# Retiming the per-token expert row operations of a one-core PEER decoder layer, and moving half of its weight residuals from VectorE to GpSimd

## The chip, the cores and the metric

One core of one Trainium2 chip runs one decoder layer for 512 tokens in one launch. The metric is device time in microseconds (us). The kernel before takes 3232.92 us (median of 3 runs, 3228.34 to 3236.88).

Names in the text: PE is TensorE, DVE is VectorE, ACT is ScalarE, POOL is GpSimd, SP is SyncE, which issues most of the DMAs.

## The reference, cut to what matters

x is 512 tokens of 2048 floats. The layer is

- h = rmsnorm(x); z = h W_in (2048 to 4096 columns: pool, q, k, v); a pooling mixer on the first 1024 columns, dilated causal attention with partial rotary embedding on 8 heads of 128; x += concat W_out.
- x += cross attention (4 heads, 256 memory tokens).
- PEER: 8 heads of queries (h W_pq, 2048 columns) are scored against two sets of 128 keys; the 16 best of each side are combined and the best 16 pairs name 16 of 16384 experts with softmax gates. Expert e adds gate * gelu(h . w_u[e]) * w_v[e]. So every token has 128 expert rows of w_u and 128 of w_v.
- a final rmsnorm.

## The kernel before, in words

Everything is float32. A projection is done with three matmuls per weight block: weight and activation are each split in a high part (float32r) and a low part (the rest), and high*high, high*low and low*high are added up (`mm3`, lines 145 to 148). `load_w` (lines 133 to 143) loads a 128x1024 half of a weight pair by SP, makes the high part `wh` on ACT, and the low part `wl = raw - wh` on DVE, or on the engine that `lo_eng` names. `proj_one` (150) makes one 128-column chunk of a projection: two `load_w`, 48 matmuls. `proj_four` (162) makes four chunks at once.

The tokens go two ways. The 128 tokens of the first block are handled on their own, from the start up to about 405 us; their 128x128 chosen experts are then fetched as rows. For each of the 128 choices k, `dot0` (311) gathers one row of w_u per token (an indirect DMA on POOL's queue, 128 rows of 8 KB, 1 MB) and DVE multiplies it with the activation `gx` in PSUM and sums (line 314). Then `turn0` (316) applies the GELU and the gates, and `axpy0` (324) gathers 128 rows of w_v and adds them up in `gx` on DVE (line 327); `out0` normalises and writes them. The first 64 tokens of the rest go the same way with two choices per step: 64 `dot1` and 64 `axpy1` (`start1`, `turn1`, `end1` around them). The other 320 tokens go through all 16384 experts as a dense product: 128 chunks of w_u (`a_chunk`, 996; 48 matmuls of 320 columns each), GELU, a product with a dense gate matrix, and 16 groups times 16 column blocks of w_v (lines 1164 to 1200; 24 matmuls each).

Order of the stages after 405 us, as the code has it:

- z: 28 chunks of W_in (`z_chunk`, 764), 20 of them between the parts of the attention heads, 8 with the pooling mixer; the choice of experts for the first block (`picks`) is made three steps per chunk at its beginning. The rotary embedding (`rope`, 755) is one shuffle and three tensor operations on DVE.
- W_out: 16 chunks, then the cross attention: 4 chunks of W_cq and 8 loads of W_co.
- queries: 16 chunks of W_pq; after each, `score` (963) makes two-level top 16 lists on DVE (five operations for each of 3 token blocks), and `dense_h` (976) makes the activations of the dense product.
- w_u: 128 chunks. The choices for three token blocks (`pick`) run beside the first ones; then 80 gate groups (`gates`, 1092: two DVE operations, 4 matmuls, one ACT copy) are spread over chunks up to K1 = 56. All gates must be in memory before the dense gate product of chunk 56. Chunks 56 to 63 follow without gates.
- w_v: 16 groups; during the first 8 of them the other 64 chunks of w_u are done as well.

The row operations wait in one list, `queue`. Each chunk calls `behind(rate/4)` four times: it adds to `owed` and takes that many entries from the list (333 to 338). `RATE` and `XR` hold the entries per chunk: 2.2 in z (chunks 10 to 26), 2.0 in W_out, 0.5 in W_cq, 3.0 in the queries, 0.4 from chunk 20 of w_u. In w_v the rest of the list is spread evenly, 1.3 times as dense in the first half (1157 to 1159). A gathered row lies in a buffer from `row_tile` (107): two, plus those in the list `spare` (`x0` from line 724, `rowx` from line 951).

Instructions are reordered on each engine by the compiler's list scheduler, so a DVE row operation that is written beside one weight tile may stand much earlier or later in DVE's order; POOL keeps the written order from line 1037 on. Each engine then runs its instructions strictly in order. PSUM holds `gx` (half of it), two banks `pm` and two `pa`.

Of the kernel before, what the change touches and what calls it, by code (L numbers as in the profile page):

```python
# [17 lines left out]
P = 128  # L18
# [24 lines left out]
RATE = (2.2, 2.0, 3.0, 0.4)  # L43

XR = 0.25

PK, Z0, ZE = 3, 1, 27
# [17 lines left out]
def hybrid_kernel(ctx: ExitStack, tc: tile.TileContext, a: dict, out: bass.AP):  # L65
# [28 lines left out]
    r2c = const.tile([P, TR], F32, name="r2c")  # L94
    accx = const.tile([P, TR], F32, name="accx")
# [66 lines left out]
    def proj_four(tiles, xh, xl, n=TR, order=None, lo_eng=None, rate=0):  # L162
# [165 lines left out]

    gx = [None]
# [29 lines left out]
    with tc.tile_pool(name="ep", bufs=1) as ep, tc.manual_schedule(engines={mybir.EngineType.SP}):  # L359
# [333 lines left out]
        hooks_x = [{}, {}, {4: [lambda: rstd_from(r2c, accx, TR)]}, {}]  # L693
# [43 lines left out]
    with tc.tile_pool(name="ac", bufs=1, reuse_waits="tile") as ac, tc.tile_pool(name="at", bufs=2, reuse_waits="tile") as at:  # L737
# [26 lines left out]
        def z_chunk(c):  # L764
# [5 lines left out]
            on = len(zc) > Z0 + math.ceil(17 / PK) + 2 and len(zc) < ZE  # L770
            return proj_one(a["w_in"][c], hH, hL, rate=RATE[0] if on else 0)

        for h in range(HEADS):
            ps = fill["q%d" % h] if h <= 1 else z_chunk(8 + h)
            q = at.tile([P, 16 + TR], F32, name="q", bufs=1)[:, :TR]
            V.scalar_tensor_tensor(out=q, in0=ps, scalar=DH ** -0.5, in1=rx, op0=ALU.mult, op1=ALU.mult)  # L776
            rope(q)
            ps = fill["v0"] if h == 0 else z_chunk(24 + h)
            vt = tmp2k()
            V.tensor_tensor(vt, ps, rx, op=ALU.mult)  # L780
# [4 lines left out]
            S.copy(v, pt[:, :TR])  # L785
# [6 lines left out]
            for i in range(RB):  # L792
# [6 lines left out]
                V.tensor_tensor(s[:, :n], ps[:, :n], mask[:, T - n:], op=ALU.add)  # L799
# [47 lines left out]
    with tc.tile_pool(name="xt", bufs=2, reuse_waits="tile") as xt:  # L847
# [4 lines left out]
        xtmp = lambda n=TR: xt.tile([P, TR], F32, name="xtmp", bufs=2)[:, :n]  # L852

# [15 lines left out]
        def x_scores(h):  # L869
            ps = proj_one(a["w_cq_h"][h], hH, hL, rate=XR * RATE[1])  # L870
# [54 lines left out]
        for t in range(8):  # L925
            w = load_w(a["w_co"][t]) if t >= 1 else None
# [12 lines left out]
        rstd_tok(accx, TR, out=yq)  # L939
    kvp.close()  # L940
# [21 lines left out]
    with tc.tile_pool(name="pq", bufs=2) as pq:  # L962
# [33 lines left out]
    def a_chunk(j, stay=False):  # L996
        ps = proj_one(a["w_u"][j], dH, dL, ND, lo_eng=G if j >= K1 + GRP and j % 2 == 0 or K1 + GRP > j >= KP else V)
# [12 lines left out]
    with tc.tile_pool(name="tw", bufs=1, reuse_waits="tile") as tw:  # L1010
        for b in range(RB):
# [22 lines left out]
            a_until(4 * b + 4)  # L1034
# [42 lines left out]
    owed = 0.0

    with tc.tile_pool(name="gw", bufs=2, side="right", reuse_waits="tile") as gw:
# [33 lines left out]
        for j in range(first, K1):  # L1113
# [187 lines left out]
```

## Time and profile before

| what | value |
|---|---|
| median of 3 runs | 3232.92 us |
| the profiled execution, own time | 3235.51 us |
| its span, first to last instruction | 3233.7 us |
| mean granted TensorE clock | 0.959 of full speed |
| PE busy | 2954.9 us (91%) |
| DVE busy | 2501.6 us (77%) |
| ACT busy | 1290.9 us (40%) |
| POOL busy | 1045.4 us (32%) |
| moved by DMA | 912.79 MB, mean 282 GB/s |

An engine's busy time is the time in which it ran at least one instruction; DMA issues, waits and semaphores are not counted. Matmuls overlap in PE, so a matmul's own duration is longer than the time it adds; the time that one adds is found as busy time over count in a stretch in which PE never waits. The granted clock is the share of full speed at which TensorE was allowed to run: 1.00 is 2.4 GHz, 0.50 is 1.2 GHz.

### The profile page before, as it was taken

The numbers are of one execution on the slowest core, as the hardware profiler recorded it, in microseconds if no ns is written. First come the engines' busy times: TensorE is split into PE (matmuls) and PEld (weight loads), VectorE is DVE, ScalarE is ACT, GpSimd is POOL, SyncE is SP. The second block draws the span as 40 slices with busy tenths as digits, with TensorE's granted clock in tenths as the row PEclk, the third lists the DMA queues.
The fourth block names the chain that finished last, engine by engine and source line by source line (L and its number), as shares of the span: only waits on it lengthen the run. The fifth ranks groups of instructions, "written<-read, shape, count | busy, mean of one in ns | idle before, by whom it ended". The sixth has DMA issues, their size and how long they took to land.

```text
span 3233.7 us, 47332 instructions
## 1 busy us (share of the span) xinstructions
PE 2954.9 (91%) x18311; PEld 2840.1 (88%) x18311; DVE 2501.6 (77%) x3569; ACT 1290.9 (40%) x1756; POOL 1045.4 (32%) x633
## 2 busy tenths in 40 slices
PE   7989878899998669999999999999999998898997
PEld 5868677788988669999999999999999998898897
DVE  7787899996459999978954777777677777777775
ACT  5666432233363224455543333333333332232234
POOL 0000012330002210000566555555555554444542
PEclk8999989999999889999999999999999999999998
DMA  7886749995428965555677999889899999899873
GB/s 266 288 297 213 236 155 336 345 360 201 126 93 323 333 253 168 173 170 216 227 268 286 365 383 352 333 342 347 334 343 371 350 346 345 329 354 352 341 269 104
DMA packets 243521, 912.79 MB, mean 282 GB/s; under 512 B 23488, under 2 KB 85600, under 8 KB 192224
## 3 DMA queue, kind: packets, MB, share of 16 engines
q1 hardware_dynamic: 136304, 471.21, 41.5%
q0 software_dynamic: 55296, 402.68, 31.7%
q10 hardware_dynamic: 51696, 35.88, 3.6%
q8 instruction: 144, 2.36, 0.3%
q14 instruction: 81, 0.66, 0.1%
HBM read 874.22 MB, written 35.45 MB: 281 GB/s over the span
## 4 chain that ended last, share of the span: by engine, by line
PE 64%; DVE 15%; issue 12%; DMA 5%; ACT 1%; POOL 1%; ACTq 0%; SPq 0%; DVEq 0%; POOLq 0%
PE pm L146 11%; PE pm L147 10%; PE pm L148 10%; PE pa L148 9%; PE pa L146 8%; PE pa L147 8%; DVE wl L142 3%; PE pa L1104 2%; DVE rows L314 2%; PE pm L384 1%; PE pm L385 1%; PE pm L383 1%; DVE gx L327 1%; DVE wl L130 1%; DMA rows<-in_w_u_rows_dram,sidx 1%
## 5 line engine op out<-in xcount | busy, mean ns | idle before, releaser
L141 ACT ACTIVATE wh<-wraw 128x1024 fp32r<-128x1024 f32 (+1 forms) x658 | 694.4, 1060 | 1126.9 <-PE pm L147 563.4
L142 POOL TENSOR_TENSOR wl<-wraw,wh 128x1024 fp32r<-128x1024 f32 x240 | 597.8, 2496 | 1035.2 <-ACT wh L141 961.0
L148 PE MATMUL pa<-ch,wl 128*128 128x320 f32 x2048 | 644.8, 316 | 57.1 <-DVE wl L142 53.6
L142 DVE TENSOR_TENSOR wl<-wraw,wh 128x1024 fp32r<-128x1024 f32 (+1 forms) x418 | 533.9, 1279 | 207.8 <-ACT wh L141 198.2
L146 PE MATMUL pa<-ch,wh 128*128 128x320 f32 x2048 | 645.1, 315 | 19.3 <-ACT wh L141 8.8
L147 PE MATMUL pa<-cl,wh 128*128 128x320 f32 x2048 | 643.4, 314 | 0.0
L146 PE MATMUL pm<-dH,wh 128*128 128x320 f32 x2048 | 634.8, 310 | 0.7 <-ACT ga L999 0.7
L147 PE MATMUL pm<-dL,wh 128*128 128x320 f32 x2048 | 633.5, 309 | 0.0
L148 PE MATMUL pm<-dH,wl 128*128 128x320 f32 x2048 | 632.8, 310 | 0.0
L148 PEld LDWEIGHTS pa<-ch,wl 128*128 128x128 f32 x2048 | 394.1, 193 | 66.0 <-DVE wl L142 61.9
L146 PEld LDWEIGHTS pa<-ch,wh 128*128 128x128 f32 x2048 | 394.8, 193 | 22.3 <-ACT wh L141 12.1
L146 PE MATMUL pm<-hH,wh 128*128 128x384 f32 x1024 | 362.5, 354 | 36.9 <-DVE q L776 14.7
L147 PEld LDWEIGHTS pa<-cl,wh 128*128 128x128 f32 x2048 | 394.7, 193 | 0.0
L146 PEld LDWEIGHTS pm<-dH,wh 128*128 128x128 f32 x2048 | 384.4, 188 | 1.0 <-ACT ga L999 1.0
L147 PEld LDWEIGHTS pm<-dL,wh 128*128 128x128 f32 x2048 | 384.4, 188 | 0.0
L148 PEld LDWEIGHTS pm<-dH,wl 128*128 128x128 f32 x2048 | 384.0, 188 | 0.1
L147 PE MATMUL pm<-hL,wh 128*128 128x384 f32 x1024 | 357.9, 350 | 0.0
L148 PE MATMUL pm<-hH,wl 128*128 128x384 f32 x1024 | 356.5, 349 | 0.4 <-DVE wl L142 0.4
L114 POOL DMA_INDIRECT rows<-in_w_u_rows_dram,sidx x107 | 124.3, 1161 | 671.8 <-ACT t2k L804 456.3
L1179 DVE TENSOR_TENSOR xT<-pa,xT 128x320 f32<-128x320 f32 x256 | 125.2, 489 | 198.2 <-PE pa L148 183.0
L146 PEld LDWEIGHTS pm<-hH,wh 128*128 128x128 f32 x1024 | 202.5, 198 | 45.7 <-issue 25.4
L147 PEld LDWEIGHTS pm<-hL,wh 128*128 128x128 f32 x1024 | 202.2, 197 | 0.9
(404 smaller groups left out, 4544.5 us busy)
## 6 DMA issues: line engine op xcount, KB each, us to landing
wraw<-in_w_u_dram SPq DMA_DIRECT2D x256, 512.0 KB
wraw<-in_w_v_dram SPq DMA_DIRECT2D x256, 512.0 KB
wraw<-in_w_in_dram SPq DMA_DIRECT2D x64, 512.0 KB
xT<-in_w_in_f_dram SPq DMA_DIRECT2D x63, 512.0 KB
gd<-stage SPq DMA_DIRECT2D x10, 2048.0 KB
gt<-gd ACTq DMA_DIRECT2D x32, 640.0 KB
wraw<-in_w_pq_f_dram SPq DMA_DIRECT2D x32, 512.0 KB
wraw<-in_w_out_dram SPq DMA_DIRECT2D x32, 512.0 KB
```

Of the source, the lines that this page charges most:

```text
L114: G.indirect_dma_start(out=dst, out_offset=None, in_=src, in_offset=bass.IndirectOffsetOnAxis(ap=idx, axis=0))
L130: V.tensor_tensor(wl, raw, wh.bitcast(F32), op=ALU.subtract)
L141: S.activation(wh[:, c], raw[:, c], AF.Copy)
L142: (lo_eng or V).tensor_tensor(wl[:, c], raw[:, c], wh.bitcast(F32)[:, c], op=ALU.subtract)
L146: TE.matmul(ps, wh, xh, start=start, stop=False)
L147: TE.matmul(ps, wh, xl, start=False, stop=False)
L148: TE.matmul(ps, wl, xh, start=False, stop=stop)
L314: V.tensor_tensor_reduce(out=r, in0=r, in1=gx[0], op0=ALU.mult, op1=ALU.add, scale=1.0, scalar=0.0, accum_out=sact[:, k:k + 1])
L327: V.scalar_tensor_tensor(out=gx[0], in0=r, scalar=sact[:, k:k + 1], in1=gx[0], op0=ALU.mult, op1=ALU.add)
L383: TE.matmul(ps, xh, wh, start=start, stop=False)
L1104: TE.matmul(pg[:, j], u[:, 0, j], u[:, 1, j], start=True, stop=True)
L1179: V.tensor_tensor(xT[:, dd, NS:], ps[:, :ND], xT[:, dd, NS:], op=ALU.add)
```

## The change

- `behind` issues row operations inside `tc.issue_after(anchor)`: each DVE instruction of the entry must stand in DVE's order after the last `wl` that DVE made for a weight tile (until `paced` is set false at the end of the gates). POOL's gathers are not tied.
- The list begins with `dot0` x128, `turn0`, `axpy0` x128, `out0`; the second kind (`start1` to `end1`) comes behind it. Before, the 128 `axpy0` stood at the end.
- The rates: 3.0 in z for attention chunks from the tenth on, 2.2 for the 8 pooling chunks, 2.5 in W_out, 2.0 in W_cq, 0.25 in the queries and in the first 21 chunks of w_u, 1.2 in chunks 21 to 55 and for the 8 after them.
- One more row buffer in z (in the memory of `mb`, from the eleventh chunk to the first pooling chunk), and one in W_out and the cross attention.
- `lo_eng=(V, G)`: in z, W_out, W_cq, W_co (every second tile) and w_u chunks 21 to 55, POOL makes one of two `wl`. In the queries and w_u chunks 0 to 20 POOL makes all of them (before: DVE all up to chunk 39, POOL all from 40 to 63).
- The three tensor operations of `rope` and the first multiplication of `dense_h` go to POOL. q and v lose their scaling multiplication on DVE: q is copied with a scale on ACT and `rz` enters at the mask (same instruction count there), v is copied on ACT and scaled in three ACT copies after its transposes.
- `KB` = 7: 21 chunks of w_u are written beside the picks, before 12; the gates start at chunk 21 and spread over 33 chunks.

```diff
-RATE = (2.2, 2.0, 3.0, 0.4)
-XR = 0.25
-PK, Z0, ZE = 3, 1, 27
+RATE = (3.0, 2.2, 2.5, 2.0, 0.25, 1.2)
+PK, Z0 = 3, 1
-K1, U0, GE = 56, 8, 2
-KP = 40
+K1, U0, GE = 56, 0, 2
+KB = 7
...
+    anchor = [None]
...
-            (lo_eng or V).tensor_tensor(wl[:, c], raw[:, c], wh.bitcast(F32)[:, c], op=ALU.subtract)
+            i = (lo_eng or V).tensor_tensor(wl[:, c], raw[:, c], wh.bitcast(F32)[:, c], op=ALU.subtract)
+        if (lo_eng or V) is V:
+            anchor[0] = i
...
-            wh, wl = load_w(tiles[half], lo_eng)
+            wh, wl = load_w(tiles[half], lo_eng[half] if isinstance(lo_eng, tuple) else lo_eng)
...
-    queue = [lambda k=k: dot0(k) for k in range(P)]
+    queue = [lambda k=k: dot0(k) for k in range(P)] + [turn0] + [lambda k=k: axpy0(k) for k in range(P)] + [out0]
+    paced = [True]
     def behind(n):
...
         while owed >= 1 and queue:
-            queue.pop(0)()
+            with tc.issue_after(anchor[0].ins) if paced[0] else nullcontext():
+                queue.pop(0)()
...
-            V.tensor_tensor(sh, sh, sinT, op=ALU.mult)
-            V.tensor_tensor(t[0:32], t[0:32], cosT, op=ALU.mult)
-            V.tensor_tensor(t[0:32], t[0:32], sh, op=ALU.add)
+            G.tensor_tensor(sh, sh, sinT, op=ALU.mult)
+            G.tensor_tensor(t[0:32], t[0:32], cosT, op=ALU.mult)
+            G.tensor_tensor(t[0:32], t[0:32], sh, op=ALU.add)
...
-            on = len(zc) > Z0 + math.ceil(17 / PK) + 2 and len(zc) < ZE
-            return proj_one(a["w_in"][c], hH, hL, rate=RATE[0] if on else 0)
+            n = len(zc) - Z0 - math.ceil(17 / PK) - 2
+            if n == 2:
+                spare.append(alloc_mb()[:, :D])
+            if c == 0:
+                spare.pop()
+            return proj_one(a["w_in"][c], hH, hL, lo_eng=(V, G), rate=0 if n <= 0 else RATE[1] if c < 8 else RATE[0])
...
-            V.scalar_tensor_tensor(out=q, in0=ps, scalar=DH ** -0.5, in1=rx, op0=ALU.mult, op1=ALU.mult)
+            S.activation(q, ps, AF.Copy, scale=DH ** -0.5)
...
-            V.tensor_tensor(vt, ps, rx, op=ALU.mult)
+                S.copy(vt, ps)
...
-        for c, ps in enumerate(proj_four(a["w_pq4"], hH, hL, rate=RATE[2])):
+        for c, ps in enumerate(proj_four(a["w_pq4"], hH, hL, lo_eng=G, rate=RATE[4])):
...
-        ps = proj_one(a["w_u"][j], dH, dL, ND, lo_eng=G if j >= K1 + GRP and j % 2 == 0 or K1 + GRP > j >= KP else V)
+        lo = G if j < RB * KB else (V, G) if j < K1 else G if j < K1 + GRP or j % 2 == 0 else V
+        ps = proj_one(a["w_u"][j], dH, dL, ND, lo_eng=lo, rate=RATE[4] if j < RB * KB else RATE[5] if j < K1 else 0)
...
-            a_until(4 * b + 4)
+            a_until(KB * b + KB)
...
-    queue += [start1] + [lambda k=k: dot1(k) for k in range(NK)] + [turn1] + [lambda k=k: axpy1(k) for k in range(NK)]
-    queue += [end1, turn0] + [lambda k=k: axpy0(k) for k in range(P)] + [out0]
-    owed = 0.0
+    queue += [start1] + [lambda k=k: dot1(k) for k in range(NK)] + [turn1] + [lambda k=k: axpy1(k) for k in range(NK)] + [end1]
...
-            if j >= first + U0:
-                behind(RATE[3])
+    paced[0] = False
```

## Rows read from the trace of the kernel before

**Rows 1.** The page, part 4: chain that ended last, shares by engine

```profile
PE 64%; DVE 15%; issue 12%; DMA 5%; ACT 1%; POOL 1%; ACTq 0%; SPq 0%; DVEq 0%; POOLq 0%
```

**Rows 2.** Busy time by stretch: PE, PEld, DVE, ACT, POOL (instructions), clock, DMA share, GB/s

```profile
405.00:772.00 367.00, 306.84 (x1597) 284.17 (x1598) 341.57 (x544) 116.64 (x201) 92.52 (x75) 0.90 0.79 294
772.00:890.00 118.00, 117.78 (x680) 117.49 (x679) 51.83 (x60) 39.75 (x49) 0.00 (x0) 1.00 0.42 130
890.00:985.00 95.00, 91.19 (x499) 84.87 (x498) 61.11 (x112) 60.98 (x118) 0.94 (x1) 1.00 0.32 101
985.00:1217.00 232.00, 166.77 (x907) 163.40 (x906) 228.35 (x549) 66.41 (x118) 57.69 (x51) 0.86 0.83 310
1217.00:1381.00 164.00, 163.30 (x1116) 163.01 (x1115) 153.62 (x419) 67.70 (x84) 0.00 (x0) 1.00 0.54 172
1381.00:1669.00 288.00, 285.22 (x2095) 284.41 (x2095) 239.51 (x230) 158.64 (x176) 86.93 (x35) 1.00 0.60 208
...
1722.00:2668.00 946.00, 917.94 (x6162) 915.30 (x6161) 674.18 (x616) 323.15 (x391) 521.46 (x308) 0.98 0.91 349
2668.00:3100.00 432.00, 383.61 (x2465) 374.35 (x2464) 335.06 (x336) 129.12 (x159) 205.04 (x122) 0.96 0.91 342
3100.00:3234.00 134.00, 112.31 (x747) 110.42 (x745) 82.29 (x120) 56.55 (x102) 43.16 (x22) 0.91 0.47 159
```

**Rows 3.** DVE's instruction groups by shape, 985 to 1217 us (queries)

```profile
L314 DVE CUSTOM_DVE_ANT_0 rows<-rows,gx 128x2048 f32<-128x2048 f32 x28 | 65.2, 2337 | 0.0
L142 DVE TENSOR_TENSOR wl<-wraw,wh 128x1024 fp32r<-128x1024 f32 x34 | 43.0, 1268 | 1.1 <-ACT wh L141 1.0
L314 DVE CUSTOM_DVE_ANT_0 rowx<-rowx,gx 128x2048 f32<-128x2048 f32 x14 | 32.7, 2335 | 1.6 <-DMA rowx<-in_w_u_rows_dram,sidx 1.6
L314 DVE CUSTOM_DVE_ANT_0 x<-x,gx 128x2048 f32<-128x2048 f32 x13 | 30.4, 2335 | 0.0
```

**Rows 4.** PE's waits, 985 to 1217 us: total us, times, longest

```profile
PE pa L969 <- ACT qh L966: 60.5, 10, 14.9
```

**Rows 5.** DVE's instruction groups by shape, 405 to 772 us (z)

```profile
L314 DVE CUSTOM_DVE_ANT_0 rows<-rows,gx 128x2048 f32<-128x2048 f32 x47 | 107.0, 2276 | 5.6 <-DMA rows<-in_w_u_rows_dram,sidx 5.6
L142 DVE TENSOR_TENSOR wl<-wraw,wh 128x1024 fp32r<-128x1024 f32 x52 | 63.1, 1214 | 6.3 <-ACT wh L141 6.3
L314 DVE CUSTOM_DVE_ANT_0 x<-x,gx 128x2048 f32<-128x2048 f32 x25 | 57.0, 2278 | 6.5 <-DMA x<-in_w_u_rows_dram,sidx 6.5
L758 DVE TENSOR_TENSOR t2k<-t2k,sinT 32x384 f32<-32x384 f32 x16 | 8.6, 539 | 0.1
```

**Rows 6.** The page, part 3: DMA queues, share of 16 engines' span

```profile
q1 hardware_dynamic: 136304, 471.21, 41.5%
q0 software_dynamic: 55296, 402.68, 31.7%
```

**Rows 7.** POOL's waits, 405 to 772 us: total us, times, longest

```profile
POOL rows L114 <- DVE sact L314: 99.3, 36, 4.8
```

**Rows 8.** POOL's instruction groups, 3100 to 3234 us: a 384-column operation

```profile
L1205 POOL TENSOR_TENSOR xT<-xT,rf 128x384 f32<-128x384 f32 x5 | 6.4, 1319 | 15.1 <-ACT rf L206 15.1
```

**Rows 9.** ACT's instructions of line 999 (one per chunk), 1381 to 1669 us

```profile
L999 ACT ACTIVATE ga<-pm x30: 416/419/440, 1382.8 to 1660.3; 128x320 f32<-128x320 f32 x30
```

**Rows 10.** DVE's gate operations, 1400 to 1510 us (no tensor operation on POOL)

```profile
L1099 DVE TENSOR_TENSOR u<-iota,e12T 128x1024 f32<-128x1024 f32 x34 | 40.9, 1221 | 4.3 <-PE pa L1104 4.3
...
L1101 DVE TENSOR_TENSOR u<-u,gT 128x512 f32<-128x512 f32 x32 | 21.3, 688 | 0.4
```

**Rows 11.** DVE's gate operations, 1520 to 1660 us (POOL makes low parts)

```profile
L1099 DVE TENSOR_TENSOR u<-iota,e12T 128x1024 f32<-128x1024 f32 x41 | 71.8, 1768 | 15.3 <-PE pa L1104 15.3
L1101 DVE TENSOR_TENSOR u<-u,gT 128x512 f32<-128x512 f32 x41 | 48.9, 1209 | 0.7
```

**Rows 12.** POOL's low parts, 1520 to 1660 us

```profile
L142 POOL TENSOR_TENSOR wl<-wraw,wh 128x1024 fp32r<-128x1024 f32 x28 | 76.1, 2716 | 398.1 <-ACT wh L141 398.1
```

**Rows 13.** DVE's low parts, 1217 to 1381 us (picks beside w_u)

```profile
L142 DVE TENSOR_TENSOR wl<-wraw,wh 128x1024 fp32r<-128x1024 f32 x46 | 56.4, 1226 | 10.1 <-ACT wh L141 10.1
```

More of the change, by code (lines that the diff above doesn't have):

```diff
@@ L1 @@
 import math
-from contextlib import ExitStack
+from contextlib import ExitStack, nullcontext
 import numpy as np
@@ L94, in hybrid_kernel @@
     r2c = const.tile([P, TR], F32, name="r2c")
+    rz = const.tile([P, NB], F32, name="rz")[:, :RB]
     accx = const.tile([P, TR], F32, name="accx")
@@ L169, in proj_four @@
             if kk == 0:
-                w = load_w(tiles[t], lo_eng)
+                w = load_w(tiles[t], lo_eng[t % 2] if isinstance(lo_eng, tuple) else lo_eng)
             behind(rate / 4)
@@ L327, in axpy0, with out0 @@
         V.scalar_tensor_tensor(out=gx[0], in0=r, scalar=sact[:, k:k + 1], in1=gx[0], op0=ALU.mult, op1=ALU.add)
+    def out0():
+        sq, so = row_tile(), nrm.tile([P, 2], F32, name="so")
+        S.activation(sq, gx[0], AF.Square, accum_out=so[:, 0:1])
+        newton(so[:, 0:1], so[:, 1:2])
+        grow = row_tile()
+        nc.scalar.dma_start(grow, a["g_rows"][1:2, :].broadcast_to([P, D]))
+        V.scalar_tensor_tensor(out=grow, in0=gx[0], scalar=so[:, 1:2], in1=grow, op0=ALU.mult, op1=ALU.mult)
+        nc.scalar.dma_start(out_0, grow)
     gx = [None]
-    queue = [lambda k=k: dot0(k) for k in range(P)]
+    queue = [lambda k=k: dot0(k) for k in range(P)] + [turn0] + [lambda k=k: axpy0(k) for k in range(P)] + [out0]
     owed = 0.0
+    paced = [True]
     def behind(n):
@@ L692, in hybrid_kernel @@
         ahead("q1", 9)
-        hooks_x = [{}, {}, {4: [lambda: rstd_from(r2c, accx, TR)]}, {}]
+        hooks_x = [{}, {}, {4: [lambda: rstd_row(r2c, rstd_tok(accx, TR, out=rz), TR)]}, {}]
         for k in range(KD):
@@ L775, in hybrid_kernel @@
             q = at.tile([P, 16 + TR], F32, name="q", bufs=1)[:, :TR]
-            V.scalar_tensor_tensor(out=q, in0=ps, scalar=DH ** -0.5, in1=rx, op0=ALU.mult, op1=ALU.mult)
+            S.activation(q, ps, AF.Copy, scale=DH ** -0.5)
             rope(q)
-            ps = fill["v0"] if h == 0 else z_chunk(24 + h)
-            vt = tmp2k()
-            V.tensor_tensor(vt, ps, rx, op=ALU.mult)
+            vt = fill["v0"]
+            if h:
+                ps = z_chunk(24 + h)
+                vt = tmp2k()
+                S.copy(vt, ps)
             pt = pa.tile([P, 512], F32, name="pa")
@@ L784, in hybrid_kernel @@
             v = at.tile([P, TR], F32, name="v", bufs=1)
-            S.copy(v, pt[:, :TR])
+            for j in range(RB):
+                S.activation(v[:, j * P:(j + 1) * P], pt[:, j * P:(j + 1) * P], AF.Copy, scale=rz[:, j:j + 1])
             ps = fill["k0"] if h == 0 else z_chunk(16 + h)
@@ L798, in hybrid_kernel @@
                 st_ = at.tile([P, 4], F32, name="st", bufs=4)
-                V.tensor_tensor(s[:, :n], ps[:, :n], mask[:, T - n:], op=ALU.add)
+                V.scalar_tensor_tensor(out=s[:, :n], in0=ps[:, :n], scalar=rz[:, i:i + 1], in1=mask[:, T - n:], op0=ALU.mult, op1=ALU.add)
                 V.tensor_reduce(st_[:, 0:1], s[:, :n], axis=AX.X, op=ALU.max)
@@ L852, in hybrid_kernel @@
         xtmp = lambda n=TR: xt.tile([P, TR], F32, name="xtmp", bufs=2)[:, :n]
+        spare.append(xt.tile([P, D], F32, name="rowt", bufs=1))
         def x1_done(c, ps):
@@ L856, in x1_done @@
             sumsq(xtmp, accx, xT[:, c, :], c == 0, TR)
-        for c, ps in enumerate(proj_four(a["w_out4"], hH, hL, order=[4, 5, 6, 7, 0, 1, 2, 3], rate=RATE[1])):
+        for c, ps in enumerate(proj_four(a["w_out4"], hH, hL, order=[4, 5, 6, 7, 0, 1, 2, 3], lo_eng=(V, G), rate=RATE[2])):
             x1_done(c, ps)
         for c in range(4, KD):
-            x1_done(c, proj_one(a["w_out"][c - 4], hH, hL, rate=RATE[1]))
+            x1_done(c, proj_one(a["w_out"][c - 4], hH, hL, lo_eng=(V, G), rate=RATE[2]))
         for k in range(KD):
@@ L869, in x_scores @@
         def x_scores(h):
[L870 removed]
+            ps = proj_one(a["w_cq_h"][h], hH, hL, lo_eng=(V, G), rate=RATE[3])
             if h == 0:
@@ L939, in hybrid_kernel @@
         rstd_tok(accx, TR, out=yq)
+    spare.pop()
     kvp.close()
@@ L1161, in hybrid_kernel @@
             cs.append(c_chunk(GRP * order[0] + jj))
-            behind(RATE[3])
+            behind(RATE[5])
         fin = None
```

14 lines of the change are left out of this document (3 added, 11 removed).

## The prediction
> **What bounds the kernel now.** I read the chain of waits first: PE holds 64% of the path, but DVE 15% and DMA 5% [rows 1], so PE is not the bound everywhere. The table by stretch says where [rows 2]. In w_u (1217 to 1669 us) PE is busy 99% at clock 1.00: nothing can be won there, only lost. In the queries (985 to 1217 us) DVE is busy 228 of 232 us, and PE 167 us at clock 0.86; its largest wait is for the query copy that feeds the scores, 60.5 us [rows 4]. In z (405 to 772 us) DVE is busy 93%, the DMA share is 0.79, the clock 0.90. In W_out (772 to 890 us) PE never waits, DVE is 44% busy and DMA 0.42. In w_v (1722 to 3100 us) the DMA share is 0.91 and PE loses some per cent.
>
> The row operations explain this. By the rates, z should hold 37 of them, W_out and W_cq 34. The trace has 47 + 25 = 72 in z [rows 5], and the queries hold 28 + 14 + 13 = 55 [rows 3], 128 us of DVE; with these 127 of the 128 `dot0`, none is left for W_out. The scheduler pulled its 34 forward, into the stage that has no DVE time.
>
> **Prices.** PE: 118 us / 680 matmuls of 384 columns = 0.1735 us, a chunk 8.33 us; 163.3 / 1116 of 320 columns = 0.1463 us, a w_u chunk 7.02 us [rows 2]. DMA at full share: the gathers took 31.7% of 3233.7 us for 384 row operations = 2.67 us each; the weight queue 41.5% for 471 MB = 2.99 us for a chunk's 1.05 MB [rows 6]. A row operation costs DVE 2.28 to 2.34 us [rows 3, 5]; a DVE low part 1.21 to 1.27 us [rows 3, 5, 13]; a low part on POOL 2.72 us there [rows 12].
>
> POOL's low parts are not free for DVE. Without them a gate group costs DVE 1.22 + 0.69 = 1.91 us [rows 10], beside them 1.77 + 1.21 = 2.98 us [rows 11]: 41 groups lose 44 us to 28 POOL tiles, 1.56 us per tile. The Trainium skill, "SBUF — State Buffer", section "Who interferes with whom", calls this an exclusive lock: a DVE instruction with two SBUF inputs and a GpSimd instruction that reads SBUF block each other for a whole instruction. The rows agree in kind; they show a part of the 2.72 us and not all of it, and I go by 1.56. What the whole would do is rival 2.
>
> **The change, stage by stage.**
>
> *Queries.* By the new rates 4 row operations stay of 55: 51 x 2.34 = 119 us leave DVE. All 32 low parts go to POOL: 32 x 1.27 = 41 us. DVE falls from 228 to about 68 us, less the moved `dense_h` multiplications. POOL takes 32 x 2.72 = 87 us and 16 small operations at no more than 1.32 us [rows 8], 108 us in all. PE's floor is 16 x 8.33 = 133 us, with scores and the first w_u chunk about 145. I take 160, since scores still wait for their copies: **-72 us**. Bounds: -87 (the floor) to -50 (POOL's 2.72 us in the path of some tiles).
>
> *z.* Row operations go from 72 to 50 (11 chunks x 3.0 + 8 x 2.2): 22 x 2.28 = 50 us off DVE. 26 of 52 low parts leave (32 us) and 48 rope operations at 0.54 us [rows 5] (26 us); the small multiplications I cost at nothing, ACT being 32% busy. DVE falls from 342 to 234 us, plus up to 28 x 1.56 = 44 us lost to POOL. POOL gets 28 x 2.72 + 48 x 1.32 [rows 8] + 50 gathers x 1.23 (92.5 / 75) = 201 us, which fits. What is late next is DMA: the 19 chunks with rows need 19 x 2.99 + 50 x 2.67 = 190 us, at 0.91, the highest share of a long stretch [rows 2], 209 us; the 9 chunks without rows at least 75 us of PE, and the attention's own 253 matmuls and hand-overs come on top. I take 337 of 367: **-30 us**. Bounds: -65 (no hand-over shows) to +10. The last is POOL's order: a gather that waits for a free buffer, 99.3 / 36 = 2.8 us [rows 7], now has low parts and rope operations behind it.
>
> *W_out.* From no row operations to 40. DMA needs 2.99 + 2.5 x 2.67 = 9.7 us per chunk against PE's 8.33. At 0.91 to 1.0 that is 155 to 170 us for 16 chunks against 133: +22 to +37. Weights fetched ahead give some back: **+25 us**. Bounds: 0 (rows late, but nothing waits) to +45. DVE takes 40 x 2.3 = 92 us there and gives up 16 x 1.22.
>
> *Cross attention.* 8 row operations, 18 us of DVE in 95 of which 61 are busy [rows 2]; 8 low parts leave. **+3 us** (-3 to +10).
>
> *w_u.* Picks: DVE did 154 us in 164, 56 of it low parts [rows 2, 13]. Now 97 + 5 row operations (12 us), plus what 42 POOL tiles cost; the picks' instructions have two inputs about half of the time, so I take 0.8 us each, 33. DVE 142 us against PE's 21 x 7.02 = 147: hidden. Gates: chunks end every 277.5 / 29 = 9.57 us there [rows 9], so 80 groups cost PE about 74 us, 0.92 each. PE for chunks 21 to 55: 35 x 7.02 + 74 = 319 us. DVE: 80 x 1.91 = 153, 35 low parts 43, 41 row operations 95, and 35 POOL tiles x 1.56 = 55: 346 us, at the best busy share that the rows show (0.98, queries) 353. That is 34 us more than PE; two PSUM banks let PE run two chunks (14 us) ahead of the gates' end: **+20 us**. Bounds: 0 to rival 2. The cover that hid gates and low parts before (PE at 99%) is gone here. `turn0` loads x0d through SP and waits there for a row buffer, with weight loads behind it; once, within the four weight buffers, up to 5 us and inside the bounds.
>
> *w_v.* The list holds 230 entries instead of 253 (136 were taken before it, now 159). First half: 1.39 to 1.27 per block, 16 gathers fewer, 43 us of DMA time out of 946 x 0.91. PE can win 946 - 6162 x 0.1463 = 45 us at most; I take -12. Second half to 3100 us: 0.69 to 0.63, some 6 fewer, 17 us of DMA; PE can win 71; I take -13. Together **-25 us** (-60 to +5). The end hides one thing less: `end1` now comes last, and its result is transposed on PE before the last group; the list is timed to empty four blocks (14 us) earlier, so I cost it at nothing; without that cover each us late is on the path (up to 10).
>
> Sum: -72 - 30 + 25 + 3 + 20 - 25 = **-79 us** from the profiled 3235.5 = 3156.5; that execution lies 2.6 us above the median, so 3154.
>
> **Rivals.**
> 1. *The added loads hide.* W_out's rows come late without holding any low part, and gates slip into the slack: +25, +3 and +20 become 0, sum -127, 3106. For: W_out uses 0.42 of DMA. Against: POOL and DVE run in order, with low parts behind rows on both.
> 2. *DVE and POOL shut each other out* (slower). Place: z and w_u, where both now run tensor operations. Price: the POOL tile's time in full, taken at 2.4 us (2.72 less what it lost itself), instead of 1.56. Picks: 97 + 12 + 42 x 2.4 = 210 against 147, +63. Gates: 153 + 43 + 95 + 84 = 375 against 319, +56; less 14. So w_u +105. z: 234 + 28 x 2.4 + 63 = 364, -3. Sum -72 - 3 + 25 + 3 + 105 - 25 = +33: 3266. It decides from w_u +99 on. For: gates grow beside POOL's tiles [rows 10, 11]. Against: these rows show two thirds of the price, where DVE is fullest. The rule of the skill's SBUF section named above is this rival taken at its word.
> 3. *POOL's order gives it back* (no change). In z, W_out and W_cq 48 tiles have their POOL half behind gathers; 2.8 us of waiting for a buffer [rows 7], half of it reaching PE, is 67 us: 3221, and with a little more nothing is left. Against: the added buffer, and two halves of lead in `wh` and `wl`. The change would then do what it says, to no use.
>
> **How the numbers follow.** Forecast 0.54, rival 1 0.20, rival 2 0.15, rival 3 0.11. The forecast's own spread is 3105 to 3210 by the bounds of the terms, which will not all fall one way. To leave out no more than 2 in 10 the range goes below rival 1 and above rival 3: 3080 to 3235. A change within 0.3% (3223 to 3243) can't be told from none. Faster is the forecast, rival 1 and 0.02 of rival 3, whose sum lies at that edge: 0.76. The other 0.09 of rival 3 is no change. Slower is rival 2: 0.15.
>
> **What would show it.** Right: a queries stage of 150 to 170 us with DVE under 60% and PE's clock near 1; 50 row operations in z and about 40 in W_out; W_out longer than before at a DMA share above 0.85; gates at about 3 us per group beside POOL's tiles, with PE in w_u below 99%; some 225 row operations after 1722 us's counterpart instead of 250. Wrong: queries still waiting on `qh` or on POOL's `wl`; W_out still 118 to 133 us (rival 1); w_u over 100 us longer (rival 2); PE waiting for POOL's `wl` behind gathers in z (rival 3).

## The result and the profile after

The changed kernel takes 3177.77 us (median of 4 runs, 3174.37 to 3182.33) against 3233.16 us before: 55 us less, ratio 0.9835, 95% interval 0.9818 to 0.9852. The forecast was 3154 us, with a range of 3080 to 3235. The changed kernel's profiled execution has a span of 3173.6 us, 60 us less than before.

The table by stretch of the changed kernel corresponds to [rows 2] and has the same columns (PE, PEld, DVE, ACT, POOL with instructions, granted clock, DMA share, GB/s). The stretches are z, W_out, cross attention, queries, picks, gates, and the two halves of w_v.

```profile
405.00:730.00 325.00, 294.53 (x1574) 275.81 (x1575) 259.00 (x385) 120.58 (x223) 177.08 (x129) 0.93 0.72 264
730.00:873.00 143.00, 136.54 (x752) 135.29 (x751) 114.50 (x120) 48.40 (x64) 73.87 (x47) 0.98 0.90 348
873.00:986.00 113.00, 91.70 (x439) 81.14 (x438) 89.49 (x125) 52.56 (x103) 39.60 (x27) 0.89 0.64 230
986.00:1138.00 152.00, 148.80 (x875) 148.13 (x874) 96.93 (x401) 62.76 (x113) 92.14 (x51) 0.99 0.45 147
1138.00:1285.00 147.00, 120.17 (x766) 117.66 (x765) 142.62 (x365) 49.63 (x64) 88.53 (x34) 0.90 0.42 132
1285.00:1678.00 393.00, 369.79 (x2599) 365.20 (x2600) 336.10 (x302) 186.17 (x209) 192.01 (x88) 0.97 0.79 289
1749.00:2663.00 914.00, 904.81 (x6129) 902.97 (x6129) 663.24 (x631) 324.51 (x394) 490.32 (x295) 0.99 0.92 352
2663.00:3151.00 488.00, 459.92 (x3051) 452.23 (x3049) 354.82 (x392) 174.74 (x242) 218.49 (x121) 0.99 0.80 293
```

For the comparison each stage ends with a landmark that both kernels have: z with the last copy of the pooling mixer, W_out and the cross attention with their last sum into xT, the queries with the last query copy, w_u with the first block sum of w_v, w_v with its last. The first and last block sums are in this view of the instructions of one line, first the kernel before, then the changed one.

```profile
L1179 DVE TENSOR_TENSOR xT<-pa,xT x256: 476/492/493, 1746.8 to 3211.2; 128x320 f32<-128x320 f32 x128
```

```profile
L1193 DVE TENSOR_TENSOR xT<-pa,xT x256: 469/491/494, 1749.3 to 3151.3; 128x320 f32<-128x320 f32 x128
```

| stage | before, us | after, us | difference | forecast | row operations before / after |
|---|---|---|---|---|---|
| z (from 405) | 363 | 324 | -39 | -30 | 72 / 52 |
| W_out | 128 | 144 | +16 | +25 | 0 / 31 |
| cross attention | 87 | 113 | +26 | +3 | 0 / 17 |
| queries | 228 | 152 | -76 | -72 | 55 / 7 |
| w_u up to the first block of w_v | 536 | 611 | +75 | +20 | 8 / 51 |
| w_v, first to last block | 1464 | 1402 | -62 | -25 | 249 / 226 |

The differences sum to -60 us. (A row operation counts in the stage in which it starts. Of w_u's 8 and 51, 5 and 42 start before the GELU of chunk 56, so beside the picks and the gates.) The gain that was clearest in advance, the queries, came as forecast; z came a little larger; but w_u gave back as much as the queries won, and the net gain is, in size, that of w_v.

**w_u.** Three views of the changed kernel between 1138 and 1308 us: DVE's groups in the picks (busy us, mean ns), POOL's low parts, and PE's largest wait (us in total, times, longest).

```profile
L295 DVE TENSOR_TENSOR oh<-oh,ecand 128x800 f32<-128x800 f32 x24 | 45.3, 1922 | 0.0
L293 DVE TENSOR_TENSOR oh<-iota,cf 128x800 f32<-128x800 f32 x24 | 40.4, 1717 | 0.0
L296 DVE TENSOR_REDUCE eid<-oh 128x16 f32<-128x800 f32 x24 | 22.6, 971 | 0.0
```

```profile
L144 POOL TENSOR_TENSOR wl<-wraw,wh 128x1024 fp32r<-128x1024 f32 x36 | 99.9, 2787 | 69.5 <-ACT wh L143 69.5
```

```profile
PE pa L1054 <- DVE e L1052: 20.8, 3, 11.0
```

The two products with two inputs in SBUF take 1.92 and 1.72 us beside POOL's low parts; the reduction, with one input, 0.97. Before (1217 to 1381 us), without POOL, the same three took 0.99 us each:

```profile
L291 DVE TENSOR_TENSOR oh<-oh,ecand 128x800 f32<-128x800 f32 x24 | 23.0, 996 | 0.0
L289 DVE TENSOR_TENSOR oh<-iota,cf 128x800 f32<-128x800 f32 x24 | 22.8, 990 | 0.0
L292 DVE TENSOR_REDUCE eid<-oh 128x16 f32<-128x800 f32 x24 | 22.8, 989 | 0.0
```

The 48 products lose 40 us; these are means, and the last section shows what they are made of. PE's order holds the transposes of each token block's picks at a fixed place, so PE waits for them (three times, 20.8 us in all), its granted clock is 0.90 in the mean of the stretch, and it does 766 matmuls in 147 us where w_u's price [rows 2] allows 147 / 0.1463 = 1005: it is some 5 chunks behind when the gates begin.

**Cross attention.** The split of the activations, a DVE operation with two SBUF inputs, grew from 618 ns to 1115 in the mean; first the kernel before (896 to 983 us), then the changed one (873 to 986 us).

```profile
L213 DVE SCALAR_TENSOR_TENSOR hL<-xT,gains,hH 128x384 fp32r<-128x384 f32 x21 | 12.5, 618 | 0.2 <-ACT hH L212 0.2
```

```profile
L217 DVE SCALAR_TENSOR_TENSOR hL<-xT,gains,hH 128x384 fp32r<-128x384 f32 x20 | 22.0, 1115 | 3.8 <-ACT hH L216 3.8
L318 DVE CUSTOM_DVE_ANT_0 rows<-rows,gx 128x2048 f32<-128x2048 f32 x9 | 20.5, 2276 | 0.0
L318 DVE CUSTOM_DVE_ANT_0 x<-x,gx 128x2048 f32<-128x2048 f32 x5 | 11.4, 2273 | 0.0
L318 DVE CUSTOM_DVE_ANT_0 rowt<-rowt,gx 128x2048 f32<-128x2048 f32 x4 | 9.1, 2274 | 0.0
```

And 17 row operations start there (the 18th of the view reaches in from W_out), where the rates write 8. Of W_out's 40, only 31 start in W_out and two in z, so seven ran late. The other two were written in the queries: up to there the rates write 98, and 100 have started when the cross attention ends. In the queries DVE makes no low part, so the tie holds their row operations only behind the last low part that DVE makes before them, in the cross attention; there these two stand, between the last splits:

```profile
959.31 1.21 DVE L144 TENSOR_TENSOR wl<-wraw,wh 128x1024 fp32r<-128x1024 f32 x1
960.44 2.28 DVE L318 CUSTOM_DVE_ANT_0 rows<-rows,gx 128x2048 f32<-128x2048 f32 x1
...
962.65 2.28 DVE L318 CUSTOM_DVE_ANT_0 x<-x,gx 128x2048 f32<-128x2048 f32 x1
...
964.85 1.90 DVE L217 SCALAR_TENSOR_TENSOR hL<-xT,gains,hH 128x384 fp32r<-128x384 f32 x1
```

### The profile page after: what moved, and what is told of

It reads as the page before. It is cut to its first block, busy times and chain, and to the rows that moved or that the text cites. A ratio compares the mean times of both kernels' runs of the same rounds, so it can differ in the third digit from the quotient of the medians.

```text
span 3173.6 us, 47405 instructions
## 1 busy us (share of the span) xinstructions
PE 2947.7 (93%) x18311; PEld 2832.5 (89%) x18311; DVE 2422.7 (76%) x3360; ACT 1298.6 (41%) x1789; POOL 1433.8 (45%) x826
## 4 chain that ended last, share of the span: by engine, by line
PE 66%; DVE 20%; DMA 5%; issue 5%; ACT 2%; POOL 0%; ACTq 0%; POOLq 0%; DVEq 0%; SPq 0%
PE pm L150 11%; PE pm L152 11%; PE pm L151 11%; PE pa L152 9%; PE pa L150 9%; PE pa L151 9%; DVE wl L144 2%; DVE u L1114 2%; DVE oh L295 1%; DVE oh L293 1%; PE pm L400 1%; PE pm L401 1%; PE pm L399 1%; PE pa L1119 1%; DMA rows<-in_w_v_rows_dram,sidx 1%
## 5 line engine op out<-in xcount | busy, mean ns | idle before, releaser
L144 POOL TENSOR_TENSOR wl<-wraw,wh 128x1024 fp32r<-128x1024 f32 x369 | 930.5, 2526 | 1433.3 <-ACT wh L143 1401.4
L152 PE MATMUL pa<-ch,wl 128*128 128x320 f32 x2048 | 634.5, 312 | 25.4 <-DVE wl L144 23.5
L152 PE MATMUL pm<-dH,wl 128*128 128x320 f32 x2048 | 640.6, 313 | 6.1 <-DVE wl L144 3.9
L150 PE MATMUL pa<-ch,wh 128*128 128x320 f32 x2048 | 636.7, 311 | 7.3 <-DVE xT L1193 4.7
L151 PE MATMUL pa<-cl,wh 128*128 128x320 f32 x2048 | 635.3, 310 | 0.0
L144 DVE TENSOR_TENSOR wl<-wraw,wh 128x1024 fp32r<-128x1024 f32 (+1 forms) x289 | 377.4, 1308 | 166.5 <-ACT wh L143 158.7
L152 PEld LDWEIGHTS pa<-ch,wl 128*128 128x128 f32 x2048 | 387.1, 189 | 30.4 <-DVE wl L144 28.1
L151 PEld LDWEIGHTS pa<-cl,wh 128*128 128x128 f32 x2048 | 388.1, 190 | 0.0
L150 PE MATMUL pm<-hH,wh 128*128 128x384 f32 x1024 | 355.9, 348 | 10.4 <-DVE k L811 3.4
L152 PEld LDWEIGHTS pm<-hH,wl 128*128 128x128 f32 x1024 | 197.6, 193 | 13.4 <-DVE wl L144 12.5
```

The source lines that it names most:

```text
L144: i = (lo_eng or V).tensor_tensor(wl[:, c], raw[:, c], wh.bitcast(F32)[:, c], op=ALU.subtract)
L150: TE.matmul(ps, wh, xh, start=start, stop=False)
L151: TE.matmul(ps, wh, xl, start=False, stop=False)
L152: TE.matmul(ps, wl, xh, start=False, stop=stop)
```

## The experiments

All ratios are against the kernel before, measured beside each run; intervals are 95%. Unless said otherwise an edit is made to the changed kernel.

**Low parts of the picks back on DVE.**

```diff
-        lo = G if j < RB * KB else (V, G) if j < K1 else ...
+        lo = V if j < RB * KB else (V, G) if j < K1 else ...
```

> Low parts of w_u chunks 0 to 20 go back to DVE. w_u up to chunk 56 takes 540 us after the change, 474 before. Theory A (POOL's low parts block the picks' two-input operations, which are late for the transposes that PE's order already holds; PE waits 21 us for them there): the picks' 128x800 products fall from 1.82 us to 0.99, PE's wait for the transposes nearly goes, w_u shortens by 20 to 40 us, total 3138 to 3158. Theory B (the 41 row operations in the gates fill DVE, the picks only shift what is hidden): the products fall too, but w_u stays within 10 us of 540, since DVE then has 51 us more of low parts; total 3170 to 3185.

Measured: 3189.76 us, ratio 0.9865 (0.9832 to 0.9897). The table by stretch, picks and then gates, and DVE's groups in the picks:

```profile
1136.00:1324.00 188.00, 181.99 (x1236) 180.65 (x1235) 179.91 (x431) 74.87 (x95) 25.82 (x15) 1.00 0.61 201
1324.00:1668.00 344.00, 314.25 (x2199) 308.67 (x2198) 326.20 (x287) 162.58 (x183) 173.35 (x75) 0.97 0.80 297
```

```profile
L144 DVE TENSOR_TENSOR wl<-wraw,wh 128x1024 fp32r<-128x1024 f32 x45 | 59.3, 1320 | 7.9 <-ACT wh L143 7.9
L295 DVE TENSOR_TENSOR oh<-oh,ecand 128x800 f32<-128x800 f32 x23 | 24.3, 1076 | 0.0
L293 DVE TENSOR_TENSOR oh<-iota,cf 128x800 f32<-128x800 f32 x24 | 22.9, 980 | 0.0
```

The products are back at 1.0 us, PE runs through the picks at clock 1.00, and chunk 56 of w_u is reached after 478 us instead of 540. So the mechanism of theory A is there. But nothing is won: the last gate group starts 532 us after the queries' end, 528 in the changed kernel. PE arrives earlier, and DVE, which has the low parts to do again, is 95% busy in the gates. Chunk 56 was the wrong landmark; the gates' end counts, and by it theory B holds. The total lies 5 us above theory B's range, with w_v at 1431 us instead of 1402.

**No row operations in the gates.**

```diff
-        ps = proj_one(..., rate=RATE[4] if j < RB * KB else RATE[5] if j < K1 else 0)
+        ps = proj_one(..., rate=RATE[4] if j < RB * KB else 0)
```

> No row operations in w_u chunks 21 to 55; the 42 go to w_v. From the end of the queries to the last gate group it is 452 us before, 528 after the change. Theory A (DVE's sum sets that end: 42 x 2.3 = 97 us less of DVE): it falls to 450 to 475 us, PE's own floor there, and w_v, if DMA bounds it, grows by 42 x 2.7 = 113 us: total 3210 to 3240. Theory B (POOL's low parts and the late picks set it): it stays above 505 us; total above 3260.

Measured: 3272.99 us, ratio 1.0136 (1.0112 to 1.0159). The last gate group comes 487 us after the queries' end: 41 us less, between the two theories; the total lies above theory A's range. w_v, with 267 row operations instead of 226, takes 1539 us instead of 1402. In the table by stretch, the picks and the gates:

```profile
1134.00:1281.00 147.00, 119.11 (x764) 116.75 (x762) 142.62 (x364) 49.36 (x63) 89.35 (x34) 0.93 0.44 132
1281.00:1621.00 340.00, 335.80 (x2425) 335.77 (x2426) 209.66 (x234) 170.29 (x195) 105.26 (x41) 0.99 0.56 189
```

Now PE is the bound of the gates (99%), still carrying what it lost in the picks (119 of 147 us).

**Both edits at once.** The two diffs above together.

> Both edits at once: w_u's first 21 chunks have their low parts on DVE, and chunks 21 to 55 no row operations. From the end of the queries to the last gate group it is 528 us after the change, 532 with the first edit alone, 488 with the second alone, 452 before. Theory A (two causes, the later one counts: PE falls 6 chunks behind while it waits for transposes of late picks, and row operations fill DVE in the gates): with both gone it is 445 to 465 us. Theory B (something else, as the even spread of low parts over both engines in the gates): it stays at 480 us or more. The total is no better than 3240, since w_v gets 42 more row operations.

Measured: 3228.37 us, ratio 0.9995 (0.998 to 1.0011); from the queries' end to the last gate group 449 us, theory A.

```profile
1133.00:1302.00 169.00, 166.54 (x1137) 165.99 (x1136) 160.90 (x420) 69.40 (x89) 10.91 (x6) 1.00 0.54 173
1302.00:1582.00 280.00, 280.00 (x2059) 279.62 (x2058) 225.57 (x230) 154.59 (x172) 78.82 (x30) 1.00 0.59 198
```

This settles w_u. The first operation of the gate groups in the four kernels (changed kernel, picks on DVE, no rows, both; the last start stands behind "to"), where the queries end at 1137.7, 1136.2, 1133.5 and 1133.0 us:

```profile
L1114 DVE TENSOR_TENSOR u<-iota,e12T x80: 1208/1212/3437, 1291.7 to 1665.6; 128x1024 f32<-128x1024 f32 x80
L1114 DVE TENSOR_TENSOR u<-iota,e12T x80: 1207/1212/3440, 1343.3 to 1668.2; 128x1024 f32<-128x1024 f32 x80
L1114 DVE TENSOR_TENSOR u<-iota,e12T x80: 1210/1223/3303, 1287.2 to 1620.8; 128x1024 f32<-128x1024 f32 x80
L1114 DVE TENSOR_TENSOR u<-iota,e12T x80: 1207/1217/3411, 1313.0 to 1581.7; 128x1024 f32<-128x1024 f32 x80
```

So from the queries' end to the last gate group it is 528 us (changed kernel), 532 (picks on DVE), 487 (no rows), 449 (both). With PE on time, 42 row operations cost 83 us, 2.0 us each, nearly DVE's full price; with the rows gone, PE's lateness from the picks costs 39 us. In the changed kernel one hides behind the other, and undoing the first alone shows nothing at the gates' end. To the first block sum of w_v the four take 611, 602, 574 and 536 us, and the kernel before takes 536: with both undone the whole loss of w_u is gone, although POOL still makes half of the gates' low parts.

**Fewer row operations in W_out and the cross attention.**

```diff
-RATE = (3.0, 2.2, 2.5, 2.0, 0.25, 1.2)
+RATE = (3.0, 2.2, 1.5, 0, 0.25, 1.2)
```

> Rate in W_out 1.5 instead of 2.5, in W_cq 0 instead of 2.0: 24 row operations fewer up to the queries, and 24 more in w_v. Cross attention takes 113 us after the change, 87 before, and W_out 144 against 128. Theory A (17 of W_out's row operations slip into the cross attention and stand in DVE's order before its low parts and splits): the cross attention falls to 87 to 93 us, W_out to 128 to 135. Theory B (the half of low parts that moved to POOL is what the cross attention waits for): it stays above 105 us. In the total the 24 operations cost w_v at most 24 x 2.67 = 64 us (if DMA alone bounds it) and at least nothing: 3135 to 3200.

Measured: 3215.43 us, ratio 0.9952 (0.9938 to 0.9967), 38 us worse than the change. W_out falls to 130 us with 23 row operations, as theory A has it. The cross attention falls to 99 with 2, between the two theories: the two are those of the queries, between the last splits as before, and the splits still take 1064 ns beside POOL. No run parts these two causes.

```profile
L217 DVE SCALAR_TENSOR_TENSOR hL<-xT,gains,hH 128x384 fp32r<-128x384 f32 x22 | 23.0, 1064 | 3.8 <-ACT hH L216 3.8
```

W_out and the cross attention win 28 us by giving up 23 row operations, and w_v pays 65 for 24, so the total comes out 15 us above the expected range: in W_out and the cross attention a row operation is worth its place.

**Without the tie.**

```diff
-    paced = [True]
+    paced = [False]
```

> Row operations are not tied to a weight tile; rates, list and engines as after the change. Theory A (the tie holds W_out's operations in W_out): without it the scheduler pulls them into z, which then holds 70 to 90 instead of 52 and grows by 30 us or more, while W_out and the cross attention fall back towards 128 and 87 us; total within 30 us of 3178. Theory B (the scheduler would leave them there anyway now that POOL's order holds low parts): z keeps 50 to 60 and the total stays within 6 us of 3178.

Measured: 3173.39 us, ratio 0.9822 (0.9785 to 0.9859), not told apart from the change. z keeps 52 row operations, W_out 31, the cross attention 17: theory B. In the changed kernel the tie decides nothing for the total. The parts do differ, at equal counts: z takes 313 us instead of 324, the cross attention 101 instead of 113, and w_v 1417 instead of 1402. In the cross attention all 17 now start in its first 65 us, before the last splits. So the number of row operations alone does not set a stage's length; in the cross attention their place in DVE's order is what differs here.

**The tie alone, in the kernel before.** The edit adds `anchor`, `paced` and the `issue_after` of the change to the kernel before, and nothing else.

> The kernel before with one part of the change alone: its DVE row operations are tied behind the last weight tile of DVE, up to the end of the gates. Theory A (the tie keeps W_out's operations out of z where nothing else does): z holds 40 to 50 row operations instead of 72 and shortens by 25 to 45 us, W_out and the cross attention take 20 or more and lengthen by less; total 3195 to 3220. Theory B (the tie does nothing alone, as its absence changed nothing after the change): z keeps 65 to 72, total within 10 us of 3232.

Measured: 3195.19 us, ratio 0.9887 (0.9861 to 0.9913): 34 us less, theory A. z holds 40 row operations and takes 329 us, W_out 27, the cross attention 5, the queries 47 and 208 us. DVE's row groups in z and the table for z, W_out, cross attention and queries:

```profile
L318 DVE CUSTOM_DVE_ANT_0 rows<-rows,gx 128x2048 f32<-128x2048 f32 x27 | 61.5, 2279 | 0.0
L318 DVE CUSTOM_DVE_ANT_0 x<-x,gx 128x2048 f32<-128x2048 f32 x13 | 29.6, 2277 | 0.0
```

```profile
405.00:734.00 329.00, 292.94 (x1573) 274.22 (x1572) 272.66 (x471) 113.05 (x196) 45.46 (x43) 0.94 0.63 225
734.00:868.00 134.00, 131.01 (x747) 130.72 (x746) 116.36 (x125) 48.82 (x65) 35.29 (x27) 0.99 0.87 323
868.00:960.00 92.00, 84.85 (x452) 76.10 (x451) 66.06 (x113) 53.32 (x104) 6.71 (x6) 1.00 0.47 164
960.00:1168.00 208.00, 159.69 (x875) 156.44 (x874) 204.81 (x500) 64.20 (x112) 54.13 (x47) 0.90 0.87 326
```

So the tie alone brings more than half of the change's gain. Which of the other parts keeps the row operations in place when it is left out again, no run tells.

**The queries' low parts back on DVE.**

```diff
-            G.tensor_tensor(hn[:, NS:], xT[:, k, NS:], r2c[:, NS:], op=ALU.mult)
+            V.tensor_tensor(hn[:, NS:], xT[:, k, NS:], r2c[:, NS:], op=ALU.mult)
...
-... proj_four(a["w_pq4"], hH, hL, lo_eng=G, rate=RATE[4])    (and proj_one for w_pq)
+... proj_four(a["w_pq4"], hH, hL, rate=RATE[4])
```

> In the queries the low parts and the first multiplication of the dense activations go back to DVE; the 4 to 7 row operations stay. The stage takes 152 us after the change, 228 before. Theory A (the 55 row operations alone held it up): DVE has 97 + 41 + 9 = 147 us in about 155, so the stage stays at 152 to 165 us. Theory B (low parts on DVE in order behind the lists of the best 16 are the cause): the stage goes back to 185 us or more. Total 3178 to 3190 by A, above 3205 by B.

Measured: 3193.77 us, ratio 0.9889 (0.9858 to 0.992). The queries take 159 us, not 228, which is theory A: their gain is that of the row operations; POOL's part is 7 us.

```profile
967.00:1126.00 159.00, 153.91 (x911) 153.27 (x909) 126.12 (x433) 65.11 (x114) 16.99 (x11) 0.99 0.48 159
```

The total is 4 us above theory A's range; w_v is 25 us longer here. The cross attention takes 102 us with 15 row operations: the two of the queries stay out of it. How much of these 11 us is theirs is open, since POOL also makes fewer low parts beside its last splits.

**z's low parts and rope back on DVE.** `lo_eng=(V, G)` is left out in `z_chunk` and the three operations of `rope` are `V` again.

> In z all low parts and the rope go back to DVE; the rates and the number of row operations (52) stay. z takes 324 us after the change, 363 before. Theory A (both the fewer row operations and POOL's share shorten it): DVE gets 31 + 26 us back on 259 of 325, z 335 to 350 us, total 3185 to 3205. Theory B (the row operations alone): z stays within 8 us of 324. Theory C (POOL's share alone): z goes back to 355 us or more.

Measured: 3233.62 us, ratio 1.0016 (1.0003 to 1.0029). z takes 345 us (theory A): of its 39 us, 21 come from POOL's share. The other 18 belong to the rest of the change in z, of which the 20 row operations that left are the largest part of DVE's time (the moved scalings and the added buffer were not taken out alone).

```profile
405.00:750.00 345.00, 299.94 (x1570) 276.41 (x1571) 293.57 (x478) 121.56 (x223) 66.69 (x57) 0.92 0.69 255
```

The total rose by more than the forecast, 56 us over the change, of which z and w_v show 21 and 31.

**The list in the old order.** The second kind of row operation stands again behind the `dot0`, and `turn0`, `axpy0` and `out0` at the end.

> The list in the order of before (second kind behind the dot0, first block's sums last), everything else as after the change. Theory A (w_v, 1402 us from its first to its last block sum after the change and 1464 before, is shorter because it holds 17 row operations fewer): w_v stays within 20 us of 1402, total 3165 to 3195. Theory B (the order itself shortens it): w_v goes to 1425 us or more, total above 3200.

Measured: 3195.47 us, ratio 0.9888 (0.9862 to 0.9914), 18 us worse. w_v takes 1426 us with 226 row operations. Total and w_v both lie at the boundary of the two theories, and four versions that keep the new order have a w_v of 1417 to 1433 us, so this run decides for neither.

**The changed kernel again, and two versions with more row operations in the queries.**

```diff
-        ... proj_four(a["w_pq4"], hH, hL, lo_eng=G, rate=RATE[4])    (and proj_one for w_pq)
+        ... proj_four(a["w_pq4"], hH, hL, lo_eng=G, rate=1.0)        (second version: 1.5, and 0 in W_cq)
```

> The changed kernel once more, unedited, beside the two versions of this call. All theories: 3170 to 3185. It gives the spread of w_v (1402 us from first to last block sum in its first profile, 1415 to 1432 in four edits with the same number of row operations there): if a second profile also lies near 1402, the edits lengthen w_v; if it lies at 1415 to 1430, that is spread between executions.

> The queries hold 16 row operations instead of 4 (rate 1.0); the 12 come out of w_v. Theory A (w_v pays 2.7 us for each row operation, since DMA bounds it; the queries have 55 us of DVE and 80 us of DMA unused): the queries grow by 0 to 10 us, w_v shrinks by about 32 us, total 3148 to 3165. Theory B (w_v's length is PE's and its row operations are hidden): total 3178 to 3190, as the queries' DVE gets 28 us more.

> No row operations in W_cq (8 before) and 24 instead of 4 in the queries (rate 1.5). Theory A (17 row operations in the cross attention cost it 14 to 26 us; the queries take them until DVE is full): the cross attention falls to 97 to 106 us, the queries grow by 5 to 15, w_v shrinks by 12 x 2.7 us; total 3135 to 3160. Theory B (the cross attention is long because of POOL's low parts): it stays at 111 to 114; total 3155 to 3175.

Measured: the change again 3177.4 us, ratio 0.9832 (0.9814 to 0.9851), w_v 1403 us. Rate 1.0: 3171.4 us, 0.9818 (0.98 to 0.9836). Rate 1.5 and none in W_cq: 3163.77 us, **0.9787 (0.9767 to 0.9806)**, 14 us better than the change beside it and the fastest version here. Rate 1.0 is not told apart from the change (3164.95 to 3174.99 us against 3169.66 to 3179.16), and its total lies between its two theories. Cross attention and queries of the last:

```profile
874.00:975.00 101.00, 86.00 (x436) 76.22 (x435) 71.86 (x108) 51.82 (x102) 32.11 (x19) 0.97 0.49 173
975.00:1126.00 151.00, 147.58 (x874) 145.77 (x873) 136.37 (x439) 63.41 (x113) 112.37 (x70) 1.00 0.78 287
```

The queries take 27 row operations instead of 7 in the same 151 us, and the cross attention falls from 112 to 101: theory A there. But w_v does not shrink: 1413 and 1417 us with 215 row operations, and so the total is 4 us above theory A's range. What both versions win besides is w_u up to the first block of w_v: 601 and 596 us against 618 in the change beside them. No run shows why.

**What a row operation costs w_v.** All runs together, from the first to the last block sum:

| row operations that start in it | w_v, us |
|---|---|
| 215 (rate 1.0; rate 1.5) | 1413, 1417 |
| 226 (change twice; picks on DVE; no tie; queries on DVE; z on DVE; old order) | 1402, 1403; 1431; 1417; 1427; 1433; 1426 |
| 249 (before; before with the tie) | 1464, 1470 |
| 250 (fewer in W_out) | 1467 |
| 267 (no rows in gates; both edits) | 1539, 1536 |

From 226 up to 267 the price is about (1537 - 1420) / 41 = 2.9 us each (2.5 to 3.3, by which of the versions with 226 one takes), near DMA's price in the prediction (2.67 us). Between 215 and 226 no price shows. The whole stretch in the table by stretch, before and after:

```profile
1746.80:3211.20 1464.40, 1385.85 (x9189) 1373.03 (x9187) 1072.98 (x1039) 498.32 (x635) 747.56 (x437) 0.98 0.88 335
1749.30:3151.30 1402.00, 1364.72 (x9176) 1354.93 (x9175) 1018.06 (x1022) 499.12 (x636) 708.50 (x415) 0.99 0.88 332
```

DMA's share stays at 0.88 while the stretch gets 4% shorter, so the time went with DMA's. That DMA is the cause is argued from this and from the price; a row operation that leaves also takes 2.3 us off DVE, and no run parts the two. Versions with equally many row operations differ by up to 31 us, though only the old order changes the code of w_v and the change itself repeats within 1 us; what in the compiled order makes that difference stays open.

## Why the prediction was right, and where its sizes were off

The forecast's sign, its main term and its range held; the gain was 55 us, not 79. That the sum came so near is in part luck: w_u and the cross attention cost 78 us more than forecast, and the other four stages won 59 more.

*Queries*: right in size (-76 for -72) and reason. DVE fell to 97 of 152 us, and PE rose to 98% busy. The row operations did it, the largest term of the sum: 48 of them left, 112 us of DVE, and with the low parts back on DVE all of the gain but 7 us stayed.

*z*: right (-39 for -30). DVE was forecast at 234 to 278 us and is 259. Rival 3 did not show: in z PE waits for none of POOL's low parts. PE's one wait for POOL there is for the rope of the first head and ends at 411.7 us, before the stage's first row operation (497 us):

```profile
PE pa L818 <- POOL q L776: 13.3, 1, 13.3
```

*W_out and cross attention*: together +42 for +28. DMA's share in W_out is 0.90, near the forecast's 0.91, but W_out held 31 row operations, not 40, and passed the rest on. The step that failed is "+3 us" for the cross attention: 8 row operations were counted there, and 17 came, two of them between the last splits; and the splits' two SBUF inputs were not priced (20 x 0.5 = 10 us). How the +26 parts between these is not settled; with the same 17 further forward the stage took 101 us.

*w_u*: the step that failed most, +75 for +20. DVE's time in the picks was forecast at 142 us and is 142.6. But "hidden" was wrong: I compared DVE's sum with PE's and took the larger. PE stands in its order before transposes that need the picks' end, so each late pick is a wait (119 to 120 of 147 us busy). This lateness and the row operations then both fell on the gates; the four kernels show 39 and 83 us, of which 79 remain after overlap. In the gates DVE's time was near the forecast (336 us for 346), but the stretch took 393 us where 353 were forecast. Rival 2 had named the place and half of the mechanism; its +105 was too much because it charges DVE 2.4 us for each low part of POOL, and the picks' products lost 40 us to 36 of them, 1.1 us each.

*w_v*: -62 for -25. The row operations fell by 23, as the sum had it, and it put 60 us of DMA time on them; but I let PE's floor decide how much of that counts and took less than half. The stage gained 62 / 23 = 2.7 us for each, DMA's whole price. The other versions with 226 row operations won only 31 to 47 us here, so a part of the -62 is not explained by their number.

## What to carry to other kernels

Work that fills gaps must be priced where it lands: the same row operation cost 2.0 us where DVE was full, some 2.9 in w_v, where DMA's time went with it, and nothing in the queries, where 20 more of them fitted into the same time. When two causes end at the same point, undoing one can show nothing; both have to be undone, alone and together. And comparing two engines' sums is not enough where one waits at a fixed place in its order for the other's result.

## What the runs showed of the hardware that was not expected

POOL's low parts slow all the DVE operations with two inputs in SBUF that were looked at, not only the gates of [rows 10, 11]: in the mean, the picks' products go from 0.99 to 1.92 us, and the scalar-tensor-tensor of the splits from 0.618 to 1.115. These means are made of two kinds of operations. One product in the picks, before and after (minimum, median, maximum in ns), and one split of the cross attention with the low part beside it (start, length in us):

```profile
L291 DVE TENSOR_TENSOR oh<-oh,ecand x24: 984/994/1017, 1245.1 to 1367.9; 128x800 f32<-128x800 f32 x24
L295 DVE TENSOR_TENSOR oh<-oh,ecand x24: 976/1148/3206, 1165.6 to 1285.4; 128x800 f32<-128x800 f32 x24
```

```profile
975.65 2.40 POOL L144 TENSOR_TENSOR wl<-wraw,wh 128x1024 fp32r<-128x1024 f32 x1 [8.07 <-ACT wh L143]
976.11 2.36 DVE L217 SCALAR_TENSOR_TENSOR hL<-xT,gains,hH 128x384 fp32r<-128x384 f32 x1 [0.92 <-ACT hH L216]
```

A product that meets no low part takes its 0.98 us; one that is caught takes up to 3.2. The split, 0.61 us when alone, starts 0.46 us into the low part and ends 0.42 us after it: it is held until POOL is done, not slowed. So the prediction's 1.56 us per low part, and the 1.1 us of the picks, are means over low parts that meet such an operation and those that do not. The row operations, whose second input lies in PSUM, keep their time through all of it, though 45 of the 128 on rows of w_u run beside a low part of POOL; their durations in the whole changed kernel (minimum, median, maximum in ns):

```profile
L318 DVE CUSTOM_DVE_ANT_0 rows<-rows,gx x66: 2256/2278/2289, 497.4 to 1486.7; 128x2048 f32<-128x2048 f32 x66
```

The Trainium skill, "SBUF — State Buffer", section "Who interferes with whom", draws the line there: two SBUF inputs contend with a GpSimd instruction that reads SBUF, one does not. These rows agree.
